# Value columns of a hybrid transformer trunk projected token-major, 512 columns at a time, and kept in DRAM

## The chip, the cores and the metric

The kernel runs on one core of a Trainium2 chip. The metric is the device time of one execution in microseconds (us). The engines are TensorE (PE in the profile, with PEld for its weight loads), VectorE (DVE), ScalarE (ACT), GpSimd (POOL) and SyncE (SP), which issues nearly all DMAs. Each engine works through its own queue of instructions in order.

## The reference

Two layers over 512 latent and 256 context tokens of width 2048. The layers share one shape; layer 1 needs the context tokens only where latent tokens read them (recurrent gates and values, attention keys and values).

```python
h  = rms_norm(x, norm_w) * (1.0 + scale[:, None]) + shift[:, None]   # shift, scale, gate = silu(c) @ ada_w + ada_b
hc = rms_norm(xc, norm_w) * (1.0 + scale_c) + shift_c
(a_u, a_v, a_z, b_q, b_i, b_ff, b_fb, b_z, c_q, c_k, c_v, c_z) = split_columns(h @ w_in)
y_a = gmlp_branch(a_u, a_v, a_z, g_ln_w, g_ln_b, g_ws, g_bs)      # 4 heads of 128; gelu, layer norm, mixing over tokens
y_b = hgrn_output(ox_f + flip(ox_b), b_z, h_norm_w)               # 4 recurrent heads, forward and backward, values b_i
y_c = diff_output(o_lat, c_z, subln_w, lam_init)                  # 4 heads of differential attention, values c_v (256 wide)
y = jnp.concatenate([y_a, y_b, y_c], axis=-1) @ w_out
x_new = x + gate[:, None] * y
```

After the second layer comes a final RMS norm. All values are float32.

## The kernel before, in words

**Numbers.** Every float32 operand of a projection is split into a high and a low part of the type fp32r (`hi`, `lo` for activations; `wh`, `wl` for weights), and a product is three matmuls: hi·wh, lo·wh, hi·wl. Splitting is a copy on ACT (L318) and a subtraction on DVE (L319) for each weight tile of 128 x 512. The activations of a layer stay in SBUF as 16 k-tiles (`hi0` to `hi15`, `lo0` to `lo15`), each 128 features by 768 tokens.

**Jobs.** The input projection is cut into jobs of one column tile (128 columns of `w_in`). `Proj` keeps the weights stationary and streams the tokens, 512 and then 256 columns at a time: 16 k-tiles x 3 products x 2 widths, 96 matmuls (L148). A recurrent head (`Hgrn`) has five jobs: two gates, query, output gate and value `bi`. An attention head (`Attn`) has eight: two each of `cz`, `ck`, `cv`, `cq`. Gated MLP (`Gmlp`) has ten: four `au`, two for its values, four `az`. Its two value jobs are of another kind, `TokProj` (L374): activations stationary, weights moving 256 wide, so that the result has tokens on the partitions. The values of the recurrent heads and of attention come out of `Proj` with features on the partitions and are turned by six transposes on PE for each column tile (`transpose_all`, L497), copied and split.

**Order.** The first four jobs (`LEAD`) run together while the activations are being made; the rest run one after another, with the next job's weights fetched ahead. Behind the projections of head 0 of the recurrent unit run its seven *levels* (`Hgrn.levels`): for each, ACT copies keys (L569), PE does 24 (layer 0) or 16 (layer 1) small matmuls (L581; the trace counts each twice), DVE merges them (L590) and scales queries (L599), POOL scales keys (L601, L603) and totals (L604). Then `mix` (L636 to L667) combines scores, states and values, and `finish` transposes the result. Tile gives each engine one fixed order of instructions, made when the program is built.

**Buffers.** PSUM has two pairs of banks under the tag `pp` (one `Proj` each) and four single banks under the tag `a1`, for which everything small queues up: levels, mix, transposes, the filler's last matmul. `wh` and `wl` have five buffers each, `adas` two.

**Fillers.** The modulation vectors of later layers are worked out on DVE beside the projections (`ada_dve`): a block is 16 steps of two operations (L275, L277), a transpose, a reduction (`red`) and four small matmuls on PE (L288). After each job `advance` lets some steps through: `FILL` per kind of unit.

Of the kernel before, what the change touches and what calls it, by code (L numbers as in the profile page):

```python
# [47 lines left out]
def trunk(  # L48
    ctx: ExitStack,
    tc: tile.TileContext,  # L50
    xT, cc, ada_w, w_in, w_out, ws, bs, pack, rope, out,
# [288 lines left out]
    def tok_weights(src):  # L340
        out = []
        for g in range(8):
            raw = wp.tile([P, 2, 2, P], F32, tag="raw", bufs=5, name=nm("raw"))
            load(
                raw.rearrange("p c k n -> p c (k n)"),
                src[:, :, 2 * g : 2 * g + 2, :].rearrange("c p k n -> p c (k n)"),
            )
            wh = wp.tile([P, 2, 2 * P], F32R, tag="wh", bufs=5, name=nm("wh"))
            wl = wp.tile([P, 2, 2 * P], F32R, tag="wl", bufs=5, name=nm("wl"))
            split_into(  # L350
                wh.rearrange("p k (c n) -> p k c n", c=2),
                wl.rearrange("p k (c n) -> p k c n", c=2),
                raw.rearrange("p c k n -> p k c n"),
            )
            out.append((wh, wl))
        return out

    class TokProj:
        def __init__(self, nch):
            self.nch = nch  # L360
            self.banks = [(0, 4, ps.tile([P, 4, 2 * P], F32, tag="pp", bufs=2, name=nm("pp")))]
            if nch > 4:
                self.banks.append((4, 6, p_one([P, 2, 2 * P])))

        def mm(self, ws, acts):
            for g, (wh, wl) in enumerate(ws):
                for k in range(2):
                    kt = 2 * g + k
                    hi, lo = acts[kt]
                    for a, b, bank in self.banks:  # L370
                        for c in range(a, b):
                            cs = slice(c * P, (c + 1) * P)
                            for i, (x, w) in enumerate(((hi, wh), (hi, wl), (lo, wh))):
                                PE.matmul(  # L374
                                    bank[:, c - a, :],
                                    x[:, cs],
                                    w[:, k, :],
                                    start=(kt == 0 and i == 0 and c % 2 == 0),
                                    stop=(kt == KT - 1 and i == 2),
                                    skip_group_check=True,  # L380
                                )
# [18 lines left out]
    yscr = [[dp.tile([P, T], F32, tag=f"y{l}_{j}", name=f"y{l}_{j}") for j in range(12)] for l in range(DEPTH)]  # L400
    xscr = [dp.tile([P, T], F32, tag=f"x1_{j}", name=f"x1_{j}") for j in range(KT)]
# [283 lines left out]
    class Attn:  # L685
# [4 lines left out]
        def jobs(self):  # L690
            h = 2 * self.hd
            out = []
            for key, ctxn, fn in (("cz", False, self.out_gate), ("ck", True, self.key), ("cv", True, self.value), ("cq", False, self.query)):
                if False:
                    out.append((COL[key] + h, ctxn, fn, "tok"))
                    continue
# [511 lines left out]
```

## Time and profile before

| | |
|---|---|
| time, median of three runs | 2842.38 us (2838.59 to 2842.87) |
| profiled execution, own time | 2844.0 us |
| its span | 2842.1 us |
| PE busy | 2774.2 us (98%) |
| PEld, DVE, ACT, POOL busy | 85%, 56%, 34%, 11% |
| chain that ended last | PE 91%, of it L148 into pp 73% |
| DMA queue of SP | 313.27 MB, 38.1% of 16 engines' span |

The span is what the trace shows; some 1.9 us of the execution lie around it. A busy share counts a matmul from start to its modelled end, and matmuls overlap, so the time that a matmul costs in a dense stream is the distance from its start to the next one's. The chain follows the work back from the last instruction; where it names PE, PE was neither idle nor waiting.

### The profile page before, as it was taken

Reading aid. Unit: us, or ns where it says so; the run is one execution under the profiler, and the core shown is the slowest. Engines: PE = TensorE matmul, PEld = TensorE weight load, DVE = VectorE, ACT = ScalarE, POOL = GpSimd, SP = SyncE. Lnnn points to the kernel's source line nnn. Section 1 sums busy time; section 2 is a strip of 40 time slices with the busy share of each in tenths; the row PEclk is TensorE's granted clock in tenths of the full one; section 3 lists DMA queues with packets and bytes.
Section 4 is the critical chain, followed back from the end, with each engine's and each line's share of the span. In section 5 each row is a group of like instructions: output and inputs, shape, how many; then the busy total and the mean of one; then the engine's idle time right before and its main releaser. Section 6 shows DMA issues by size and latency. Waiting matters only on the chain.

```text
span 2842.1 us, 47179 instructions
## 1 busy us (share of the span) xinstructions
PE 2774.2 (98%) x18724; PEld 2401.6 (85%) x18724; DVE 1587.5 (56%) x3256; ACT 963.5 (34%) x1855; POOL 325.7 (11%) x307
## 2 busy tenths in 40 slices
PE   5989999999999999999999999999999999999997
PEld 3678888888888888898888888888888888889786
DVE  4475676767767576624768664334353535344434
ACT  3243233224343343322311243333253535342321
POOL 0033023000000000001011023233000000001122
PEclk9999999999999999999999999999999999999998
DMA  9833433443333334334645422222222222324543
GB/s 357 285 96 84 121 108 107 121 126 90 116 90 115 93 98 126 93 93 121 208 145 163 121 65 67 61 67 72 67 75 64 71 67 64 78 79 137 153 97 93
DMA packets 168862, 316.29 MB, mean 111 GB/s; under 512 B 18240, under 2 KB 32704, under 8 KB 168640
## 3 DMA queue, kind: packets, MB, share of 16 engines
q1 hardware_dynamic: 168640, 313.27, 38.1%
q8 instruction: 147, 2.41, 0.3%
q14 instruction: 75, 0.61, 0.1%
HBM read 294.85 MB, written 18.35 MB: 110 GB/s over the span
## 4 chain that ended last, share of the span: by engine, by line
PE 91%; issue 3%; DVE 2%; DMA 1%; POOL 1%; ACT 1%; SPq 0%; DVEq 0%; POOLq 0%; ACTq 0%
PE pp L148 73%; PE pp L374 3%; PE a L808 3%; PE a L769 2%; PE a L497 2%; PE a L148 2%; PE a L250 1%; PE a L374 1%; PE a L581 1%; PE a L659 1%; PE a L636 1%; POOL A L601 0%; POOL A L603 0%; DMA T<-y 0%; PE a L883 0%
## 5 line engine op out<-in xcount | busy, mean ns | idle before, releaser
L148 PE MATMUL pp<-hi,wh 128*128 128x512 f32 (+1 forms) x4016 | 1392.5, 348 | 5.5 <-ACT hi L311 2.8
L148 PE MATMUL pp<-lo,wh 128*128 128x512 f32 (+1 forms) x4016 | 1396.7, 348 | 0.5 <-DVE lo L312 0.2
L148 PE MATMUL pp<-hi,wl 128*128 128x512 f32 (+1 forms) x4016 | 1389.1, 346 | 0.0
L148 PEld LDWEIGHTS pp<-hi,wh 128*128 128x128 f32 x4016 | 759.5, 190 | 108.0 <-ACT hi L311 5.6
L148 PEld LDWEIGHTS pp<-lo,wh 128*128 128x128 f32 x4016 | 761.2, 190 | 99.0 <-issue 6.5
L148 PEld LDWEIGHTS pp<-hi,wl 128*128 128x128 f32 x4016 | 760.2, 189 | 90.6
L319 DVE TENSOR_TENSOR wl<-raw,wh 128x512 fp32r<-128x512 f32 x634 | 451.0, 713 | 675.6 <-ACT wh L318 653.7
L318 ACT CAST wh<-raw 128x512 fp32r<-128x512 f32 x634 | 392.3, 621 | 1192.6 <-PE pp L148 996.6
L277 DVE SCALAR_TENSOR_TENSOR acc<-adas,cc_s,acc 128x256 f32<-128x256 f32 x960 | 430.7, 498 | 72.2 <-DMA adas<-in_ada_w_dram 71.3
L817 POOL TENSOR_TENSOR ars<-e,mhalf 128x1 f32<-128x1 f32 x40 | 24.7, 617 | 1249.2 <-DVE e L815 1249.2
L780 ACT ACTIVATE C<-a,nb 128x256 f32<-128x256 f32 (+1 forms) x144 | 80.6, 566 | 54.5 <-DVE nb L776 47.7
L774 DVE TENSOR_REDUCE mx<-a 128x1 f32<-128x256 f32 (+1 forms) x144 | 72.7, 538 | 27.4 <-PE a L769 27.2
L808 PE MATMUL a<-A,WT 128*128 128x256 f32 x624 | 87.7, 282 | 0.0
L808 PEld LDWEIGHTS a<-A,WT 128*128 128x128 f32 x624 | 83.1, 191 | 3.8
L769 PE MATMUL a<-K,Q 128*128 128x256 f32 (+1 forms) x432 | 85.5, 336 | 0.0
L145 POOL TENSOR_TENSOR WT<-WT,T 128x768 f32<-128x768 f32 (+1 forms) x26 | 42.1, 1619 | 367.8 <-ACT T L144 367.8
L569 ACT COPY T<-A 128x768 f32<-128x768 f32 (+1 forms) x56 | 43.8, 782 | 95.2 <-POOL A L603 92.3
L769 PEld LDWEIGHTS a<-K,Q 128*128 128x128 f32 x432 | 68.1, 189 | 8.5
L705 ACT COPY T<-pp 32x512 f32<-32x512 f32 x128 | 74.1, 579 | 1.9
L374 PE MATMUL pp<-wh,hi 128*128 128x256 f32 x256 | 73.4, 287 | 0.1
L374 PE MATMUL pp<-wh,lo 128*128 128x256 f32 x256 | 73.1, 286 | 0.0
L374 PE MATMUL pp<-wl,hi 128*128 128x256 f32 x256 | 73.1, 286 | 0.0
(226 smaller groups left out, 2314.0 us busy)
## 6 DMA issues: line engine op xcount, KB each, us to landing
raw<-in_w_in_dram SPq DMA_DIRECT2D x512, 256.0 KB, 2.9
adas<-in_ada_w_dram SPq DMA_DIRECT2D x256, 256.0 KB, 2.9
raw<-in_w_out_dram SPq DMA_DIRECT2D x128, 256.0 KB, 3.0
adaw<-in_ada_w_dram SPq DMA_DIRECT2D x42, 384.0 KB, 7.1
K<-in_ada_w_dram SPq DMA_DIRECT2D x28, 384.0 KB, 6.6
T<-y SPq DMA_DIRECT2D x12, 384.0 KB, 4.9
A<-in_xT_dram SPq DMA_DIRECT2D x8, 384.0 KB, 6.0
B<-in_xT_dram SPq DMA_DIRECT2D x8, 384.0 KB, 6.3
```

The lines of the kernel that those rows point to most:

```text
L148: i = PE.matmul(*args, **kw)
L277: V.scalar_tensor_tensor(acc[:, i, :], wt[:, kt % 2, :], sca, acc[:, i, :], op0=ALU.mult, op1=ALU.add)
L318: S.copy(hi, src)
L319: V.tensor_tensor(lo, src, hi.bitcast(F32), op=ALU.subtract)
L374: PE.matmul(bank[:, c - a, :], x[:, cs], w[:, k, :], start=(kt == 0 and i == 0 and c % 2 == 0), stop=(kt == KT - 1 and i == 2), skip_group ...
L497: PE.transpose(pt[:, c - a, :], src[:, c * P : (c + 1) * P], ident)
L569: S.copy(km[:, :n].rearrange("p (j h i) -> p j h i", h=2, i=m), view(K2, 0, [[2 * m, n // (2 * m)], [T + m, 2], [1, m]]),)
L705: S.copy(sw[a : a + 32, :LAT], p[b : b + 32, :LAT])
L769: PE.matmul(pt[:, : hi - lo], a[:, qs], b[:, k0 + lo : k0 + hi], start=(i == 0), stop=(i == 2))
L774: V.tensor_reduce(mx[:, i : i + 1], pt[:, : hi - lo], axis=AX.X, op=ALU.max)
L780: S.activation(pr[:, m, lo:hi], pt[:, : hi - lo], AF.Exp, bias=nb, scale=SCALE, accum_out=sums[:, m, i : i + 1] if len(parts) == 2 else sm ...
L808: PE.matmul(po, a[:, c, :], b[:, c0 + c, :], start=(cnt == 0), stop=(cnt == 3 * nkc - 1))
```

## The change

The 16 value column tiles of a layer that belong together in fours are no longer jobs. `TOK` lists the first column tile of four *groups*: `bi` of the four recurrent heads, the first and second half of `cv`, and `av`. A `TokGroup` has activations stationary and weights moving 512 wide (L365 after the change), with one PSUM bank for each chunk of 128 tokens: six (four for gated MLP in layer 1). Two of the six are `a1` banks, four are the two `pp` pairs. It goes through 12 k-tiles chunk by chunk, then through the last four (`TOKLAST`) for one chunk after another. `store` copies each bank to SBUF on ACT (for gated MLP with Gelu) and writes it to DRAM. The four groups run behind the lead and the levels of head 0, before all other jobs. The units load their values from there later, and the six transposes of each value column go. The mix of head 0 now comes in the program behind group 0, and `prepare_rest` too. Of the fillers 24, 40, 40 and 40 steps are let through after the groups (`TOKFILL`), and `FILL` for a recurrent job is 7. The swap of the first two remaining jobs is gone. The lines after L147 have other numbers: 288, 319, 497, 554 and 581 of before are 289, 320, 498, 553 and 580 there.

```diff
+TOK = (16, 48, 52, 4)
...
-    class TokProj:
+    class TokGroup:
         def __init__(self, nch):
             self.nch = nch
-            self.banks = [(0, 4, ps.tile([P, 4, 2 * P], F32, tag="pp", bufs=2, name=nm("pp")))]
-            if nch > 4:
-                self.banks.append((4, 6, p_one([P, 2, 2 * P])))
+            self.banks = [p_one([P, 512]) for _ in range(nch - 4)]
+            for _ in range(2):
+                pair = ps.tile([P, 2, 512], F32, tag="pp", bufs=2, name=nm("pp"))
+                self.banks += [pair[:, 0, :], pair[:, 1, :]]
 
         def mm(self, ws, acts):
...
+            steps = [(kt, c) for kt in range(KT - TOKLAST) for c in range(self.nch)]
+            steps += [(kt, c) for c in range(self.nch) for kt in range(KT - TOKLAST, KT)]
+            for kt, c in steps:
+                hi, lo = acts[kt]
+                wh, wl = (w.rearrange("p c n -> p (c n)") for w in ws[kt])
+                cs = slice(c * P, (c + 1) * P)
+                for i, (x, w) in enumerate(((hi, wh), (hi, wl), (lo, wh))):
+                    PE.matmul(
+                        self.banks[c],
+                        x[:, cs],
+                        w,
...
+        def store(self, scr, func):
+            for c, bank in enumerate(self.banks):
+                t = g3("T3")
+                if func == AF.Copy:
+                    S.copy(t[:, :512], bank)
+                else:
+                    S.activation(t[:, :512], bank, func)
+                load(scr[:, c, :], t[:, :512])
...
-        def value(self, p):
-            raw = g3("T3")
-            p.act(raw, AF.Copy, T)
-            self.vt = vt = g3("K3", shape=(P, NCH, P))
-            for a, b, pt in transpose_all(raw, NCH):
-                V.tensor_copy(vt[:, a:b, :], pt[:, : b - a, :])
+        def last(self, p):
+            self.out_gate(p)
+            self.value()
+
+        def value(self):
+            self.vt = g3("K3", shape=(P, NCH, P))
+            load(self.vt, tscr[self.L.l][0][:, :, self.hd * P : (self.hd + 1) * P])
             self.mix()
             self.finish()
...
         def query(self, p, m):
             self.q[m] = self.rotate(p, self.L.n, "Q3")
+            if m == 0:
+                self.value()
...
         rest = jobs[LEAD:]
-        if SWAP:
-            rest[0], rest[1] = rest[1], rest[0]
-        nxt = fetch(rest[0])
+        nxt = tok_weights(w_tok[l, 0])
...
         u0.levels()
+        for i in range(4):
+            pt = TokGroup(NCH if i < 3 else L.nch)
+            pt.mm(nxt, acts)
+            nxt = tok_weights(w_tok[l, i + 1]) if i < 3 else fetch(rest[0])
+            pinned[0] = False
+            pt.store(tscr[l][i], AF.Copy if i < 3 else AF.Gelu)
+            if i == 0:
+                u0.value()
+                if l == 0:
+                    prepare_rest()
+            advance(fillers, TOKFILL[i])
```

How the change moves instructions is shown at three places. The numbers behind names tell buffers apart; `a1_`, `pp_` are PSUM banks, `wh_`, `wl_` weights, `hi`, `lo` activations.

First place: PE, levels of head 0 in layer 1. Before, around level 2 (L581):

```order
L148 MATMUL pp_2828_17649<-hi11_2758_17235,wl_2793_17409 128x256
L148 MATMUL pp_2828_17649<-hi12_2773_17286,wh_2795_17414 128x512
L581 MATMUL a1_2811_17486<-C6_2803_17436,T3_2810_17484 32x32 x16
L148 MATMUL pp_2828_17649<-lo12_2774_17287,wh_2795_17414 128x512
L148 MATMUL pp_2828_17649<-hi12_2773_17286,wl_2796_17415 128x512
L148 MATMUL pp_2828_17649<-hi13_2776_17313,wh_2795_17414 128x512
```

Between one level and the next stand some 24 matmuls of a job there. After the change, levels 1 to 6 (L580), the transposes of the keys (L498) and the first matmul of group 0 into an `a1` bank:

```order
L365 MATMUL pp_2855_17088<-wh_2786_16784,lo4_2714_16387 128x512
L580 MATMUL a1_2835_16922<-C6_2827_16872,T3_2834_16920 32x32 x16
L580 MATMUL a1_2837_16946<-C6_2827_16872,T3_2836_16944 32x32 x16
L580 MATMUL a1_2839_16970<-C6_2827_16872,T3_2838_16968 32x32 x16
L580 MATMUL a1_2841_16994<-C6_2827_16872,T3_2840_16992 32x32 x16
L580 MATMUL a1_2843_17021<-C6_2827_16872,T3_2842_17019 32x32 x16
L580 MATMUL a1_2845_17048<-C6_2827_16872,T3_2844_17046 64x64 x8
L498 MATMUL a1_2847_17064<-ident_75,A6_2822_16855 128x128 x4
L498 MATMUL a1_2848_17065<-ident_75,A6_2822_16855 128x128 x2
L498 MATMUL a1_2850_17075<-ident_75,A6_2822_16855 128x128 x4
L498 MATMUL a1_2851_17076<-ident_75,A6_2822_16855 128x128 x2
L365 MATMUL a1_2852_17085<-wh_2774_16760,hi0_2661_16171 128x512
```

Levels 1 to 6 now follow one another with nothing between. Ahead of these rows stand 60 matmuls of the group (k-tiles 0 to 4 into the four `pp` banks), 18 of them between level 0 and level 1. Layer 0 has the same picture: 24 matmuls, level 0, 25, level 1, 11, then levels 2 to 6 and the transposes.

Second place: PE, group 3 of layer 0. After the change, the end of its first 60 matmuls, the matmuls of two filler blocks (L289) and its first into an `a1` bank; the same form stands in group 2, with one block in place of two:

```order
L365 MATMUL pp_632_3538<-wh_556_3294,hi4_133_668 128x512
L365 MATMUL pp_632_3538<-wl_557_3295,hi4_133_668 128x512
L365 MATMUL pp_632_3538<-wh_556_3294,lo4_134_669 128x512
L289 MATMUL a1_611_3445<-red_610_3443,fold_80 32x4 x4
L289 MATMUL a1_623_3504<-red_622_3502,fold_80 32x4 x4
L365 MATMUL a1_629_3535<-wh_544_3270,hi0_77_374 128x512
L365 MATMUL a1_629_3535<-wl_545_3271,hi0_77_374 128x512
```

Before, a filler block's matmul (L288) stood among the matmuls of a job that need nothing of it, as here in layer 0:

```order
L148 MATMUL pp_537_3305<-hi14_259_1351,wh_525_3262 128x256
L497 MATMUL a1_508_3110<-ident_75,WT_493_3064 128x128 x4
L497 MATMUL a1_509_3111<-ident_75,WT_493_3064 128x128 x2
L288 MATMUL a1_531_3274<-red_530_3272,fold_80 32x4 x4
L148 MATMUL pp_537_3305<-lo14_260_1352,wh_525_3262 128x256
L148 MATMUL pp_537_3305<-hi14_259_1351,wl_526_3263 128x256
```

The second of the L289 reads `red_622`, the last row of the next fence. DVE's queue at the same place, after the change (L278 is L277 of before): the second of the two blocks, `acc_612`.

```order
L278 SCALAR_TENSOR_TENSOR acc_612_3451<-adas_613_3452,cc_s_86,acc_612_3451 128x256
L211 TENSOR_TENSOR adaT0_94<-a1_611_3445,pack_98 128x4
L278 SCALAR_TENSOR_TENSOR acc_612_3451<-adas_613_3452,cc_s_86,acc_612_3451 128x256
L278 SCALAR_TENSOR_TENSOR acc_612_3451<-adas_614_3458,cc_s_86,acc_612_3451 128x256 x4
L278 SCALAR_TENSOR_TENSOR acc_612_3451<-adas_615_3464,cc_s_86,acc_612_3451 128x256 x4
L278 SCALAR_TENSOR_TENSOR acc_612_3451<-adas_616_3470,cc_s_86,acc_612_3451 128x256 x4
L278 SCALAR_TENSOR_TENSOR acc_612_3451<-adas_617_3476,cc_s_86,acc_612_3451 128x256 x4
L278 SCALAR_TENSOR_TENSOR acc_612_3451<-adas_618_3482,cc_s_86,acc_612_3451 128x256 x4
L278 SCALAR_TENSOR_TENSOR acc_612_3451<-adas_619_3488,cc_s_86,acc_612_3451 128x256 x4
L278 SCALAR_TENSOR_TENSOR acc_612_3451<-adas_620_3494,cc_s_86,acc_612_3451 128x256 x4
L284 STREAM_TRANSPOSE T3_621_3500<-acc_612_3451 128x512
L286 TENSOR_REDUCE red_622_3502<-T3_621_3500 128x16
```

Ahead of these rows, and behind `wl_557` (the split of weight tile 4 of group 3), stands the first block, `acc_600`, in the same form: 32 operations, a transpose, a reduction. `wl_557` takes the buffer of `wl_504`, weight tile 15 of group 2. Before, the 32 operations of a block stood in twos, threes and fours among the work of a job:

```order
L277 SCALAR_TENSOR_TENSOR acc_532_3280<-adas_535_3293,cc_s_86,acc_532_3280 128x256 x2
L644 SCALAR_TENSOR_TENSOR Q3_492_3058<-Q3_492_3058,K3_422_2478,a1_490_3051 128x128
L277 SCALAR_TENSOR_TENSOR acc_532_3280<-adas_536_3299,cc_s_86,acc_532_3280 128x256 x2
L319 TENSOR_TENSOR wl_540_3405<-raw_538_3402,wh_539_3404 128x512
L277 SCALAR_TENSOR_TENSOR acc_532_3280<-adas_536_3299,cc_s_86,acc_532_3280 128x256 x2
L277 SCALAR_TENSOR_TENSOR acc_532_3280<-adas_550_3428,cc_s_86,acc_532_3280 128x256 x3
```

Third place: PE, the end of the mix of head 0 in group 1 of layer 0, after the change. Ahead of it stand 60 matmuls of the group and the mix's own; L498 transposes the mix's result, L425 and L289 belong to `prepare_rest` and to a filler block:

```order
L659 MATMUL a1_421_2282<-K3_402_2218,K3_321_1543 128x128
L659 MATMUL a1_421_2282<-Q3_405_2227,C6_319_1539 128x128
L498 MATMUL a1_424_2292<-ident_75,WT_409_2246 128x128 x4
L498 MATMUL a1_425_2293<-ident_75,WT_409_2246 128x128 x2
L425 MATMUL a1_427_2311<-lpr_426_2309,ones_82 128x2
L425 MATMUL a1_430_2321<-lpr_429_2319,ones_82 128x2
L289 MATMUL a1_447_2397<-red_446_2395,fold_80 32x4 x4
L365 MATMUL a1_453_2428<-wh_349_2106,hi0_77_374 128x512
```

`K3_402` are the values that the mix loads from DRAM. Before, the matmuls of a job stood between the mix and its transposes.

## Rows read from the trace of the kernel before

**Rows 1.** The page, parts 1 and 4: engines' busy time, chain by engine.
```profile
PE 2774.2 (98%) x18724; PEld 2401.6 (85%) x18724; DVE 1587.5 (56%) x3256; ACT 963.5 (34%) x1855; POOL 325.7 (11%) x307
...
PE 91%; issue 3%; DVE 2%; DMA 1%; POOL 1%; ACT 1%; SPq 0%; DVEq 0%; POOLq 0%; ACTq 0%
```
**Rows 2.** Windows: stretch, length, engines' busy us, granted clock, DMA share, GB/s.
```profile
139.14:142.55 3.41, 3.41 (x16) 1.36 (x10) 0.69 (x1) 0.62 (x1) 0.00 (x0) 0.50 0.90 324
1207.51:1210.92 3.41, 3.41 (x17) 3.08 (x17) 1.35 (x5) 3.38 (x7) 0.00 (x0) 0.50 0.47 120
160.00:215.00 55.00, 46.81 (x597) 40.03 (x597) 45.77 (x80) 23.93 (x43) 23.07 (x22) 1.00 0.40 122
1690.00:1740.00 50.00, 50.00 (x504) 42.60 (x503) 21.60 (x33) 20.43 (x40) 28.60 (x25) 1.00 0.28 65
```
**Rows 3.** Waits of PE: in total, times, longest (us).
```profile
PE a L581 <- DVE C L599: 5.8, 3, 2.5
PE a L250 <- DMA B<-in_ada_w_dram: 2.3, 1, 2.3
PE a L822 <- DVE ao L819: 2.1, 1, 2.1
```
**Rows 4.** Timeline of PE, 700 to 712: start, length, instruction, idle before.
```profile
700.33 0.39 PE L148 MATMUL pp<-hi,wl 128*128 128x512 f32 x1
...
702.61 0.28 PE L148 MATMUL pp<-hi,wh 128*128 128x256 f32 x1
...
704.04 0.40 PE L148 MATMUL pp<-hi,wh 128*128 128x512 f32 x1
...
704.74 0.82 PE L497 MATMUL a<-ident,C 128*128 128x128 f32 x6
...
705.62 0.39 PE L148 MATMUL pp<-lo,wh 128*128 128x512 f32 x1
```
**Rows 5.** Timeline of PE, 1215 to 1219.
```profile
1214.72 0.28 PE L374 MATMUL pp<-wh,lo 128*128 128x256 f32 x1
...
1217.85 0.28 PE L374 MATMUL pp<-wl,hi 128*128 128x256 f32 x1
```
**Rows 6.** The page, part 6: DMA issues, KB each, us from issue to landing.
```profile
adas<-in_ada_w_dram SPq DMA_DIRECT2D x256, 256.0 KB, 2.9
...
T<-y SPq DMA_DIRECT2D x12, 384.0 KB, 4.9
...
y<-WT SPq DMA_DIRECT2D x4, 384.0 KB, 2.5
```
**Rows 7.** Timeline of ACT in the levels of layer 1.
```profile
1718.57 0.62 ACT L569 COPY T<-A 128x512 f32<-128x512 f32 x1 [1.98 <-POOL A L603]
```
**Rows 8.** Timeline of POOL, the same level.
```profile
1719.51 0.84 POOL L601 TENSOR_TENSOR A<-A,K 128x384 f32<-128x384 f32 x1
1720.31 0.84 POOL L603 TENSOR_TENSOR A<-A,K 128x384 f32<-128x384 f32 x1
```
**Rows 9.** Timeline of POOL in the levels of layer 0.
```profile
178.38 0.98 POOL L601 TENSOR_TENSOR A<-A,B 128x384 f32<-128x384 f32 x1
179.32 1.10 POOL L603 TENSOR_TENSOR A<-A,B 128x384 f32<-128x384 f32 x1
```
**Rows 10.** Timeline of ACT, the same level.
```profile
180.45 0.84 ACT L569 COPY T<-A 128x768 f32<-128x768 f32 x1 [1.32 <-POOL A L603]
```
**Rows 11.** Timeline of PE, mix of head 0 in layer 0.
```profile
223.73 2.39 PE L636 MATMUL a<-K,Q 128*128 128x128 f32 x20
...
245.61 0.82 PE L497 MATMUL a<-ident,WT 128*128 128x128 f32 x6
```
**Rows 12.** Timeline of DVE, filler operations of a later block.
```profile
442.56 1.67 DVE L277 SCALAR_TENSOR_TENSOR acc<-adas,cc_s,acc 128x256 f32<-128x256 f32 x4
445.18 1.67 DVE L277 SCALAR_TENSOR_TENSOR acc<-adas,cc_s,acc 128x256 f32<-128x256 f32 x4 [0.95 <-DMA adas<-in_ada_w_dram]
```
**Rows 13.** Groups of DVE: count, busy us, mean ns, idle before.
```profile
L283 DVE STREAM_TRANSPOSE T<-acc 128x512 f32<-128x512 f32 x32 | 22.6, 705 | 0.3
```

More of the change, by code (lines that the diff above doesn't have):

```diff
@@ L50, in trunk @@
     tc: tile.TileContext,
[L51 removed]
+    xT, cc, ada_w, w_in, w_tok, w_out, ws, bs, pack, rope, out,
 ):
@@ L341, in tok_weights @@
         out = []
[L342 to L355, printed above, removed]
+        for kt in range(KT):
+            raw = wp.tile([P, 4, P], F32, tag="raw", bufs=5, name=nm("raw"))
+            load(raw.rearrange("p c n -> p (c n)"), src[kt])
+            out.append(w_split(raw))
@@ L365, in mm @@
         def mm(self, ws, acts):
[L366 to L381, printed above, removed]
+            steps = [(kt, c) for kt in range(KT - TOKLAST) for c in range(self.nch)]
@@ new lines, in mm @@
+            steps += [(kt, c) for c in range(self.nch) for kt in range(KT - TOKLAST, KT)]
[8 more added lines that the diff above has]
+                        w,
+                        start=(kt == 0 and i == 0),
+                        stop=(kt == KT - 1 and i == 2),
+                        skip_group_check=True,
+                    )
@@ L400, in trunk @@
     yscr = [[dp.tile([P, T], F32, tag=f"y{l}_{j}", name=f"y{l}_{j}") for j in range(12)] for l in range(DEPTH)]
+    tscr = [[dp.tile([P, NCH, 512], F32, tag=f"t{l}_{g}", name=f"t{l}_{g}") for g in range(4)] for l in range(DEPTH)]
     xscr = [dp.tile([P, T], F32, tag=f"x1_{j}", name=f"x1_{j}") for j in range(KT)]
@@ L509, in jobs @@
                 (COL["bq"] + h, False, self.query),
-                (COL["bz"] + h, False, self.out_gate),
+                (COL["bz"] + h, False, self.last),
             ]
-            out.append((COL["bi"] + h, True, self.value))
-            return out
         def gate(self, p, d):
@@ L692, in jobs @@
             out = []
[L693 to L696, printed above, removed]
+            for key, ctxn, fn in (("cz", False, self.out_gate), ("ck", True, self.key), ("cq", False, self.query)):
                 for m in range(2):
@@ L832, in jobs @@
         def jobs(self):
-            v = [(COL["av"] + 2 * j, False, lambda p, j=j: self.value(p, j), "tok") for j in range(2)]
             u, z = (
@@ L904, in up @@
             p.act(self.u[h], AF.Gelu, n)
+            if h == 0:
+                self.value()
+            if h == 3:
+                self.mix()
         def out_gate(self, p, h):
@@ L945, in run_layer @@
         lead = jobs[:LEAD]
-        is_tok = lambda j: len(j) > 3
-        fetch = lambda j: tok_weights(w_in[l, j[0] : j[0] + 2]) if is_tok(j) else weights(w_in[l, j[0]])
+        fetch = lambda j: weights(w_in[l, j[0]])
         pts = []
@@ L997, in run_layer @@
         u0.levels()
[L998 to L1005 removed]
+        for i in range(4):
[9 more added lines that the diff above has]
+            advance(fillers, TOKFILL[i])
+        for i, j in enumerate(rest):
+            pt = Proj(width(j))
+            for g in range(4):
+                mm_group(pt, nxt[g], acts, g)
             nxt = fetch(rest[i + 1]) if i + 1 < len(rest) else weights(w_out[l, 0])
@@ L1162, in wtiles @@
         return w.reshape(l, k // P, P, n // P, P).transpose(0, 3, 2, 1, 4)
+    w_in = wtiles(a["w_in"])
+    w_tok = np.stack([w_in[:, c : c + 4] for c in TOK], 1).transpose(0, 1, 4, 3, 2, 5)
     small = dict(
```

69 lines of the change are left out of this document (24 added, 45 removed).

## Prediction

> **What bounds the kernel now.** I read the page first: its engine line and its chain say that TensorE (PE) is nearly all there is [rows 1]. PE is busy for 98% of the span, and 91% of the chain that ended last is PE work. So a change counts in two ways only: by the time that its matmuls take in the stream, and by new waits of PE. The busy column can't price the first, since matmuls overlap; I take distances between starts in the timeline. For the second I read which stretches have gaps today. Between 160 and 215 us, where head 0 of the recurrent unit runs its seven levels in layer 0, PE lacks 55.00 − 46.81 = 8.2 us; the same place of layer 1 (1690 to 1740) has no gap at all [rows 2]. Those gaps are short (three of them 5.8 us together) and wait for VectorE's (DVE's) C of L599 [rows 3]: a level's matmuls come due before the chain behind them is ready. Nearly everything else runs dense, so a chain that loses its cover of matmuls will show in full.
>
> **What the change removes on PE.** Ten matmuls of 512 columns start 702.61 − 700.33 = 2.28 us apart, 0.228 us each; twelve of 256 take 704.04 − 702.61 = 1.43 us, 0.119 each [rows 4]. The token-major 256s of before (L374) take (1217.85 − 1214.72)/26 = 0.120 [rows 5]; between the two rows shown lie 25 of their kind. Before, 12 value columns a layer (4 bi, 8 cv) cost 48 matmuls of each width, 1152 of each over both layers, and gated MLP 16 × 3 × 2 × (6 + 4) = 960 of 256. After, 16 × 3 × (24 + 22) = 2208 of 512 do the same. So 1056 more of 512 at 0.228 (+240.8) and 2112 fewer of 256 (1152 × 0.119 + 960 × 0.120 = 252.3): **−11.5 us**. If the weights as moving side ran at 0.230, it would be −9.4. The value transposes go: 24 groups of six. Such a group lies at 704.74; from 704.04 to 705.62 are 1.58 us for four matmuls of 512 columns, which take 0.92 without it, so 0.66 us each [rows 4], 24 × 0.66 = **−15.8 us**. Together −27.
>
> The Trainium skill ("TensorE: Matmul & The Clock Gate", section "Back-to-back issue gap") has a start-to-start time of columns/2.4 GHz + 2.5 ns, so 216 ns for 512 and 109 for 256; an estimate by that page is 1056 × 0.216 − 2112 × 0.109 = −2 us for the first term, and a sum 9 us higher. The trace has 228 and 119 instead, so halving the count pays more here.
>
> **What it adds off PE.** ScalarE copies banks out and casts weights either way, DVE splits either way; neither is near full (34% and 56% [rows 1]), so I cost them at nothing as long as PE has matmuls to run. A store of 384 KB lands 2.5 us after issue, a load of 384 KB from the same kind of scratch after 4.9 [rows 6]. For heads 1 to 3, attention and gated MLP the loads are asked for at least a job ahead or have the next job's 96 matmuls (48 × 0.347 = 16.7 us) as cover: nothing. If that cover were gone, each would cost some 5 to 10 us.
>
> **What it moves: six places.** A group needs two banks of the tag a1 besides the four of pp, and the order shows that they are handed out behind all earlier users of a1. Until then PE has only the four pp banks, and with five weight buffers only k-tiles 0 to 4: 60 matmuls, 13.7 us. What stands ahead of the first a1 matmul in PE's queue holds all the rest.
>
> *Levels, layer 1.* Levels 2 to 6 and the transposes stand with no matmul between them. One turn is a copy on ScalarE (0.62 [rows 7]) and two products on GpSimd (0.84 each [rows 8]), some 2.45 us with the handovers. From level 0 six turns (14.7) and a tail of one copy and two products (2.3) make 17; cover is 18 matmuls (4.1) and the levels' own matmuls (some 2): **+11 us**. Below, 6 (the products run two turns ahead, as they may); above, 16 (cover lost).
>
> *Levels, layer 0.* A turn is 0.84 + 0.98 + 1.10 and handovers, 3.05 us [rows 9, 10]; 6 × 3.05 + 2.9 = 21.2, less 36 matmuls (8.2) and the levels' own (3), are 10 us of gaps where there are 8.2 today: **+2 us**. Bounds −3 (no DVE filler stands between the levels now, and that made some of today's gaps) and +8.
>
> *Mix of head 0, layer 0,* now in group 1. Banks copied out, store 2.5, load 4.9: the values are there some 9 to 10 us after group 0. From the mix's first matmul to the transposes of its result are 21.9 us today (223.73 to 245.61 [rows 11]) with matmuls between; 16 filler operations still stand between its DVE steps, so I take 20. That is 30 us against 60 matmuls and the mix's own (19 in all): **+11 us**, between 6 (the matmuls that stretched the chain are gone) and 14.
>
> *Mix, layer 1.* No filler there: 16 × 0.42 = 6.7 us less of chain: **+3 us**, 0 to 6.
>
> *Group 2, layer 0.* The small matmul L289 of a whole filler block stands ahead of its a1 banks, and DVE does that block behind the split of weight tile 4, which waits for group 1's end. A filler pair of k-tiles (four operations) takes 1.67 us on DVE, and 445.18 − 442.56 = 2.62 where it waits for its load [rows 12]; two buffers and a load of 2.9 us [rows 6] allow 2.2 to 2.6. Eight pairs, two of them loaded already: 6 × 2.4 + 2 × 1.7 + transpose, reduction and split (2.8) = 20.6, less 13.7: **+7 us**; 3 with DVE alone, 8 with every load late.
>
> *Group 3, layer 0.* Two whole blocks stand there, acc_600 and acc_612, again behind weight tile 4 (wl_557): 64 operations. With DVE alone 16 × 1.67 + two transposes and reductions (0.7 each [rows 13], 2.8) + 0.7 = 30.2; with 2.3 a pair 40. I take 38, nearer the rows with loads, since stores and weights now stand in the same queue: 38 − 13.7 = **+24 us**, bounds 14 and 27.
>
> Waits: 11 + 2 + 11 + 3 + 7 + 24 = 58.
>
> *The clock.* After waits of 2.1 and 2.3 us (L822, L250 [rows 3]) TensorE had stretches of 3.41 us at half clock (1.2 GHz), granted 0.50 (139.14 and 1207.51), but none in 160 to 215, where it waited 2.5 us and resumed [rows 2]. A stretch costs half of itself, 1.7 us; five new waits above 3 us: **+9**, between 0 and 17 (double stretches).
>
> The Trainium skill says in the same page (section "Loop structure matters more than you think") that long waits between matmuls drop the clock, which speaks against this change; the rows at 139 and 1207 agree with it, the row of 160 to 215 shows that not every wait does it.
>
> **Sum.** −27 + 58 + 9 = +40 us on the profiled execution, 2844.0 (span 2842.1 and 1.9 around it): 2884. That execution lies 1.6 us above the median of 2842.38, so 2882. Low bounds: waits −3 + 6 + 6 + 0 + 3 + 14 = 26, clock 0, net −1. High: 8 + 16 + 14 + 6 + 8 + 27 = 79, clock 17, net +69.
>
> **Rivals.** 0.2%, 5.7 us, is about what a measurement here tells from no change.
>
> *The waits are half as long* (chance 0.20): chains run ahead where I count them from level 0, and filler loads keep up. Waits and clock of 21 to 47: 2836 to 2862, of it 0.08 within 0.2%. For it: GpSimd's and ScalarE's steps of a level don't need PE. Against: DVE's 64 operations alone leave 16 us at group 3.
>
> *Only the removal shows* (0.13): faster. The mechanism is that DVE does the filler blocks before the groups end, so L289 finds its sums ready, and levels and mixes cost what they do now: −27 + 11 of the mixes gives 2826. It decides when all waits and clock together stay under 27 − 6 = 21. For it: DVE is busy for 56% only [rows 1]. Against: it is an in-order queue, and wl_557 there can't run before group 2 gives its buffer back.
>
> *The round trip is late* (0.05): value loads queue on SP behind stores that wait for ScalarE's copies, and attention or gated MLP wait too: one wait of 10 us in a layer more, 20 and a clock stretch each: 2905 to 2920.
>
> *The forecast* (0.62): 2862 to 2910. Faster 0.13, same 0.08, slower 0.12 + 0.62 + 0.05 = 0.79. The range 2836 to 2910 leaves out the second rival and most of the third.
>
> **What would show it.** In the profile of after: L365 starts 0.228 us apart; no value transposes; PE waits ahead of L289 for DVE's red in groups 2 and 3 of layer 0, 7 and 24 us; L580 with 2.4 to 3 us between levels 2 to 6; a wait of some 10 us at the mix of head 0; half clock behind them; from head 1 on as dense as now. It is wrong if the first a1 matmul of group 3 comes within 20 us of group 2's end, or if new waits stand in attention.

## The result, and the profile after

The changed kernel takes 2912.64 us, median of four runs (2910.09 to 2915.8), against 2841.16 for the kernel before: ratio 1.0253, 95% interval 1.0235 to 1.0271. It is 71.5 us slower. The forecast was 40 slower, and the range ended at 2910. The profiled execution has a span of 2909.1 us, 67.0 more than before, and a mean granted clock of 0.977.

The page of after, its parts 1, 2 and 4 (busy time, the span in 40 slices, chain by engine), beside [rows 1]:

```profile
PE 2769.5 (95%) x17524; PEld 2353.5 (81%) x17524; DVE 1579.1 (54%) x3224; ACT 967.7 (33%) x1852; POOL 328.5 (11%) x307
...
PE   5988997999999999999999998999999999999997
...
PEclk9989998999999999999999999999999999999998
...
PE 84%; DVE 5%; DMA 5%; issue 4%; ACT 1%; POOL 1%; SPq 0%; DVEq 0%; POOLq 0%; ACTq 0%
```

PE's busy time is hardly less, its share of the chain fell from 91% to 84%, and DVE and DMA took up the difference. The waits of PE after (in total, times, longest, us), beside [rows 3]:

```profile
PE a L289 <- DVE red L286: 34.2, 5, 17.3
...
PE a L580 <- ACT T L568: 10.2, 5, 2.6
...
PE a L580 <- DVE C L598: 7.9, 6, 1.7
PE a L498 <- DVE WT L667: 7.0, 2, 3.5
PE a L659 <- DVE Q L644: 4.5, 3, 2.3
...
PE pp L365 <- DVE T L484: 3.1, 1, 3.1
PE pp L149 <- DVE T L484: 2.9, 1, 2.9
```

The largest is the one before the filler's small matmuls (L289). In group 3 of layer 0 (timeline of PE: start, length, instruction, idle before) the 60 matmuls into pp end, and then:

```profile
439.31 0.29 PE L289 MATMUL a<-red,fold 128*32 128x4 f32 x8 [6.87 <-DVE red L286]
456.91 0.29 PE L289 MATMUL a<-red,fold 128*32 128x4 f32 x8 [17.31 <-DVE red L286]
457.12 0.80 PE L365 MATMUL a<-wh,hi 128*128 128x512 f32 x1
457.72 0.63 PE L365 MATMUL a<-wl,hi 128*128 128x512 f32 x1
458.15 0.63 PE L365 MATMUL a<-wh,lo 128*128 128x512 f32 x1
458.57 0.63 PE L365 MATMUL a<-wh,hi 128*128 128x512 f32 x1
```

24.2 us of waiting, and behind it matmuls that start 0.42 to 0.43 apart: half clock, 1.2 GHz. DVE at the same time goes through the two blocks:

```profile
443.28 3.30 DVE L278 SCALAR_TENSOR_TENSOR acc<-adas,cc_s,acc 128x256 f32<-128x256 f32 x8 [1.16 <-DMA adas<-in_ada_w_dram]
447.66 3.33 DVE L278 SCALAR_TENSOR_TENSOR acc<-adas,cc_s,acc 128x256 f32<-128x256 f32 x8 [1.08 <-DMA adas<-in_ada_w_dram]
452.09 3.29 DVE L278 SCALAR_TENSOR_TENSOR acc<-adas,cc_s,acc 128x256 f32<-128x256 f32 x8 [1.10 <-DMA adas<-in_ada_w_dram]
455.42 0.71 DVE L284 STREAM_TRANSPOSE T<-acc 128x512 f32<-128x512 f32 x1
456.17 0.69 DVE L286 TENSOR_REDUCE red<-T 128x16 f32<-128x512 f32 x1
```

Two loads' worth (eight operations) come every 4.4 us, 2.2 a pair of k-tiles: the end of the reduction at 456.86 lets PE go on at 456.91.

Windows of after, over the six places (length, then PE's busy us first; the granted clock is the third number from the end):

```profile
172.80:204.15 31.35, 24.53 (x432) 20.22 (x433) 23.04 (x26) 11.38 (x22) 24.25 (x22) 0.79 0.16 49
267.90:290.10 22.20, 13.53 (x79) 12.13 (x77) 14.54 (x42) 2.46 (x14) 1.34 (x1) 0.76 0.21 65
350.00:365.00 15.00, 8.13 (x49) 6.24 (x48) 12.07 (x30) 0.00 (x0) 0.00 (x0) 0.89 0.40 123
425.60:457.20 31.60, 7.41 (x51) 5.84 (x46) 25.94 (x64) 0.00 (x0) 0.00 (x0) 0.68 0.39 118
550.00:580.00 30.00, 23.06 (x221) 20.02 (x221) 27.47 (x51) 5.21 (x7) 7.49 (x5) 0.94 0.43 132
1760.00:1780.20 20.20, 11.56 (x274) 9.54 (x272) 7.16 (x13) 6.65 (x17) 15.16 (x19) 0.78 0.01 2
1844.00:1855.20 11.20, 7.75 (x60) 7.19 (x58) 4.82 (x16) 1.47 (x8) 1.04 (x1) 1.00 0.00 0
```

Length less busy time gives PE's idle time: levels of layer 0 6.8 (8.2 before, [rows 2]), mix 8.7, group 2 6.9, group 3 24.2; in layer 1 levels 8.6 and mix 3.4. The row at 550 is head 1's levels, with 6.9 that were not forecast.

**Where 67 us of span went.** I add up all distances between successive starts on PE from the first to the last (2808.0 us before, 2875.9 after), take out the idle time that the trace gives before an instruction (34.3 and 107.0), and count what then lies in stretches of half clock (21.2 and 76.2) by half. What is left is an estimate of PE's work at full clock: 2763 before, 2731 after. So the work fell by 32, idle time rose by 73, and half clock took some 27: together 68.

### The profile page after: what moved, and what is told of

Same layout as the page of the kernel before. It is cut to its first block, busy times and chain, and to the rows that moved or that the text cites. A ratio compares the mean times of both kernels' runs of the same rounds, so it can differ in the third digit from the quotient of the medians.

```text
span 2909.1 us, 44897 instructions
## 1 busy us (share of the span) xinstructions
PE 2769.5 (95%) x17524; PEld 2353.5 (81%) x17524; DVE 1579.1 (54%) x3224; ACT 967.7 (33%) x1852; POOL 328.5 (11%) x307
## 4 chain that ended last, share of the span: by engine, by line
PE 84%; DVE 5%; DMA 5%; issue 4%; ACT 1%; POOL 1%; SPq 0%; DVEq 0%; POOLq 0%; ACTq 0%
PE pp L149 59%; PE pp L365 8%; PE a L365 5%; PE a L802 3%; PE a L763 2%; DVE acc L278 2%; DMA adas<-in_ada_w_dram 2%; PE a L149 1%; PE a L498 1%; PE a L251 1%; DMA adaw<-in_ada_w_dram 1%; PE a L580 1%; PE a L659 1%; DMA K<-in_ada_w_dram 1%; DVE wl L320 1%
## 5 line engine op out<-in xcount | busy, mean ns | idle before, releaser
L149 PE MATMUL pp<-hi,wh 128*128 128x512 f32 (+1 forms) x3248 | 1137.1, 352 | 8.4 <-ACT hi L312 3.1
L149 PE MATMUL pp<-lo,wh 128*128 128x512 f32 (+1 forms) x3248 | 1140.3, 352 | 0.6 <-DVE lo L313 0.5
L149 PE MATMUL pp<-hi,wl 128*128 128x512 f32 (+1 forms) x3248 | 1134.3, 350 | 0.0
L149 PEld LDWEIGHTS pp<-hi,wh 128*128 128x128 f32 x3248 | 616.9, 190 | 91.8 <-ACT hi L312 4.1
L149 PEld LDWEIGHTS pp<-lo,wh 128*128 128x128 f32 x3248 | 618.5, 191 | 82.5 <-issue 4.2
L149 PEld LDWEIGHTS pp<-hi,wl 128*128 128x128 f32 x3248 | 617.6, 190 | 76.1 <-issue 0.5
L278 DVE SCALAR_TENSOR_TENSOR acc<-adas,cc_s,acc 128x256 f32<-128x256 f32 x960 | 434.0, 502 | 78.7 <-DMA adas<-in_ada_w_dram 77.9
L365 PE MATMUL pp<-wh,hi 128*128 128x512 f32 x512 | 199.3, 392 | 3.1 <-DVE T L484 3.1
L365 PE MATMUL pp<-wl,hi 128*128 128x512 f32 x512 | 200.4, 391 | 0.0
L365 PE MATMUL pp<-wh,lo 128*128 128x512 f32 x512 | 200.3, 391 | 0.0
L365 PEld LDWEIGHTS pp<-wh,hi 128*128 128x128 f32 x512 | 96.6, 189 | 23.4 <-issue 3.3
L365 PEld LDWEIGHTS pp<-wl,hi 128*128 128x128 f32 x512 | 96.5, 189 | 20.0
L365 PEld LDWEIGHTS pp<-wh,lo 128*128 128x128 f32 x512 | 96.6, 189 | 19.9
L365 PE MATMUL a<-wh,hi 128*128 128x512 f32 x224 | 89.7, 405 | 0.0
L365 PE MATMUL a<-wl,hi 128*128 128x512 f32 x224 | 89.4, 399 | 0.0
L365 PE MATMUL a<-wh,lo 128*128 128x512 f32 x224 | 89.0, 397 | 0.0
```

The lines of the kernel that those rows point to most:

```text
L149: i = PE.matmul(*args, **kw)
L278: V.scalar_tensor_tensor(acc[:, i, :], wt[:, kt % 2, :], sca, acc[:, i, :], op0=ALU.mult, op1=ALU.add)
L365: PE.matmul(self.banks[c], x[:, cs], w, start=(kt == 0 and i == 0), stop=(kt == KT - 1 and i == 2), skip_group_check=True,)
```

## The experiments

All ratios are against the kernel before. Each edit is on the changed kernel unless said otherwise.

**e1, loads of the tables and first fillers in program order.** The SP timeline of after shows four loads among the first ones, which in the kernel before came behind the lead:

```profile
25.38 2.64 SPq L70 DMA_DIRECT2D raw<-in_w_in_dram  x4
28.68 0.33 SPq L70 DMA_DIRECT2D rope_c<-in_rope_dram  x1
29.65 0.33 SPq L70 DMA_DIRECT2D rope_s<-in_rope_dram  x1
30.69 1.47 SPq L70 DMA_DIRECT2D adas<-in_ada_w_dram  x2
```

They are the change's doing: it sets `pinned[0] = False`, which frees loads of program order, ahead of `prepare_rest` and the first `advance`, and the scheduler moves them forward.

```diff
                 if l == 0:
+                    pinned[0] = True
                     prepare_rest()
             advance(fillers, TOKFILL[i])
+            pinned[0] = False
```

> The changed kernel with one thing undone: the loads of the rope tables and of the first fillers are again kept in program order, so that the scheduler can't issue them among the first loads of the lead, where after the change four of them (1 MB) stand. Theory: they push the lead's own loads back where the DMA queue is full, and that is why the lead, whose code is the same, ends some 9.5 us later than before. Then the lead ends near 160 us again and the time is 2901 to 2905. Rival: the lead is later for another reason (scatter of the first loads, another order of its matmuls); then the time stays at 2910 to 2915 and the lead ends near 169.

Measured: 2918.5, ratio 1.0268 (1.0253 to 1.0283). Most of the lead's delay went, as the theory says, but not all: the first matmul of group 0 starts at 164.81 in place of 172.80, and the first job before the change at 161.19. The time did not follow. The first filler's loads now stand behind the store of head 0's mix, begin at 275.92 (timeline of SP, e1), and PE waits for that block ahead of group 1's a1 banks (timeline of PE, e1):

```profile
297.77 0.29 PE L289 MATMUL a<-red,fold 128*32 128x4 f32 x8 [24.22 <-DVE red L286]
```

Eight us won in the lead and 24 lost here: the same trap as in groups 2 and 3.

**e2, no fillers behind the groups.**

```diff
-    TOKFILL = (24, 40, 40, 40)
+    TOKFILL = (0, 0, 0, 0)
-    FILL = dict(Hgrn=7, Attn=7, Gmlp=4, Out=9)
+    FILL = dict(Hgrn=11, Attn=10, Gmlp=6, Out=9)
```

> The changed kernel with no filler steps behind the groups; they are spread over the later jobs instead (11, 10, 6 a job for recurrent heads, attention, gated MLP). Theory: the waits of 7 us in group 2 and of 7 + 17 us in group 3 go, and with them the half clock behind them (about 7 us); the time falls by 35 to 42 us to 2870 to 2878. Rival: DVE is short of time in the layer, the fillers' time comes back as waits in later jobs, and the time stays above 2890.

Measured: 2882.3, ratio 1.0145 (1.013 to 1.016), 30.3 us less. The waits for `red` went from 34.2 us to 1.5, as the theory says. The gain stayed 5 to 12 us short of it: the wait of the transposes for the mix (L498 for DVE's WT) rose from 7.0 to 12.3, and half clock fell only from 76.2 to 68.9 us. Neither theory alone.

**e3, levels and mix of head 0 behind the groups.**

```diff
-        u0.levels()
         for i in range(4):
...
+        u0.levels()
         for i, j in enumerate(rest):
...
+            if i == 1:
+                u0.value()
             j[2](pt)
```

> The changed kernel with the levels of head 0 behind the fourth group and its mix behind the second of the remaining jobs, in both layers; fillers as in the changed kernel. Theory: the waits between levels (some 10 us in layer 0, 8.6 in layer 1) shrink to those of before (7.5 and 0), those at the mix (8.7 and 3.4) go, and the half clock behind them too: 25 to 37 us less, 2876 to 2888. Rival 1: what counts is that the chains take as long as they do, and the waits only move to the new places: 2905 to 2915. Rival 2: the clock is lost anyway, and only the idle time comes back: 2890 to 2895.

Measured: 2884.06, ratio 1.0141 (1.0124 to 1.0158), 28.6 us less, as the theory says. The waits of L580 for ACT's copies fell from 10.2 to 1.7; those for `red` stayed (36.2).

**e4, all three.** The edits of e2 and e3, with `prepare_rest` moved behind group 3 and the tables and the fillers of the first two remaining jobs loaded in order.

```diff
+            if i == 3 and l == 0:
+                pinned[0] = True
+                prepare_rest()
+                pinned[0] = False
             advance(fillers, TOKFILL[i])
+        u0.levels()
...
             if i + 2 < len(rest):
+                pinned[0] = l == 0 and i < 2
                 advance(fillers, FILL[type(owner[i + LEAD]).__name__])
+                pinned[0] = False
```

> All three together: loads of the tables and first fillers kept in order, no fillers behind the groups, levels and mix of head 0 behind them. Theory: what is left of the change is the shorter stream on PE (27 us less by the prediction's working) and a few small waits: 2815 to 2832, faster than before. Rival: the removal is worth much less than 27 us (a 512 column matmul with moving weights costs as much as two of 256, or the stores, casts and loads take it back): 2838 to 2850, no faster than before.

Measured: 2865.19, ratio 1.008 (1.0065 to 1.0095). The theory failed: 47 us less than the changed kernel, but still 23 more than before. By the sum used above PE's work is 2825.9 − 68.6 − 53.5/2 = 2731, the same 32 us less than before, so the rival (the removal is worth little) falls too. What is left is idle time, 68.6 against 34.3, and half clock. The largest part of what is new lies in the recurrent heads (waits of PE, e4):

```profile
PE a L580 <- DVE C L598: 14.0, 8, 3.8
...
PE a L553 <- DVE WT L682: 3.7, 1, 3.7
```

Of the 14.0, 3.8 belong to head 0, whose levels e4 put above these jobs, 2.7 to head 3 of layer 1, the rest to heads 1 and 2 of layer 0. A head now has four jobs of matmuls in place of five above the same chain of levels and mix, but that alone does not make these waits: e5, below, has four jobs a head too, and waits for this C in head 3 of layer 1 alone. e4 also runs head 0's chain beside the other heads and lets 11 filler steps a job through in place of 7; e8 separates these two in part.

**e5, groups without a1 banks.** Each group goes over its weights twice, for four chunks of tokens and then for two, on the pp banks alone; all else as in the changed kernel.

```diff
     class TokGroup:
-        def __init__(self, nch):
-            self.nch = nch
-            self.banks = [p_one([P, 512]) for _ in range(nch - 4)]
-            for _ in range(2):
+        def __init__(self, a, b):
+            self.a, self.b = a, b
+            self.banks = []
+            for _ in range((b - a) // 2):
...
-        for i in range(4):
-            pt = TokGroup(NCH if i < 3 else L.nch)
+        passes = [(i, a, b) for i in range(4) for a, b in ((0, 4), (4, 6)) if i < 3 or a < L.nch]
+        for at, (i, a, b) in enumerate(passes):
+            pt = TokGroup(a, min(b, NCH if i < 3 else L.nch))
```

> The changed kernel with groups that use the pp banks alone: each group goes over its weights twice, first for four chunks of tokens, then for two, so the weights of those groups are loaded, cast and split twice; levels, mix and fillers stay where the change put them. Theory: what held PE in the first two groups and in groups 2 and 3 was that the a1 banks stand behind levels, mix and filler blocks in PE's order; without a1 the matmuls of the group stand between them, so of the 54 us of waits at the six places nearly all go, and 15 to 20 us of half clock with them; the lead stays 8 to 10 us late: 2832 to 2850. Rival: a second split of the weights takes DVE and ScalarE longer than the 22 us that two chunks give, and PE waits for wl: 2860 or more.

Measured: 2845.82, ratio 1.0016 (1.0007 to 1.0025), 67 us less than the changed kernel, with levels, mix and fillers where the change put them. That is the theory, and it settles what held PE: the order behind the a1 banks. Waits of PE, e5:

```profile
PE a L289 <- DVE red L286: 4.9, 3, 4.0
...
PE pp L365 <- DVE T L484: 3.1, 1, 3.1
...
PE a L580 <- DVE C L598: 2.7, 2, 1.7
PE pp L365 <- DVE wl L320: 2.7, 2, 2.4
```

The wait for `red` is 4.9 in place of 34.2, and the second split of the weights costs 2.7 of waiting. Half clock fell from 76.2 to 38.6 us and idle time from 107.0 to 54.2. PE's work by the sum above is 2812.8 − 54.2 − 38.6/2 = 2739, 8 more than in the changed kernel; why is open.

**e6, the same with the loads of e1.** On e5:

```diff
                 if l == 0:
+                    pinned[0] = True
                     prepare_rest()
             advance(fillers, TOKFILL[i])
+            pinned[0] = False
```

> As the one before, with the loads of the rope tables and of the first fillers kept in program order. Theory: the lead ends near 161 us as before the change, and since no a1 bank of a group waits for a filler block, nothing is held by the later filler: 8 to 10 us less than the one before, 2822 to 2842. Rival: the first filler block is late again and PE waits for it as in the first experiment: 2845 or more.

Measured: 2849.46, ratio 1.0027 (1.0017 to 1.0037): no gain. The wait of the first group fell from 3.1 to under 1, but the first filler is late again (10.4 us for `red`, 4.9 in e5), and weights too (5.2 for wl). The rival was right in kind, with a smaller wait than it said.

**e7, the price of the columns alone.** On e4, each matmul of a group as two of 256 columns.

```diff
-                    PE.matmul(
-                        self.banks[c],
+                    for hf in (slice(0, 256), slice(256, 512)):
+                        PE.matmul(
+                            self.banks[c][:, hf],
...
```

> The kernel with all three things undone (2865 us), with each matmul of a group as two of 256 columns: 4416 in place of 2208, nothing else changed. It measures the price of the columns alone. Theory: two of 256 take 2 x 0.1195 us where one of 512 takes 0.228, so 24 us more: 2885 to 2893. Rival: the width is worth next to nothing (two at 0.114): 2863 to 2872.

Measured: 2882.27, ratio 1.014 (1.0125 to 1.0155), 17.1 us more than e4: between the two. Its timeline of PE has a pair in 0.24 us:

```profile
200.26 0.40 PE L366 MATMUL pp<-wh,hi 128*128 128x256 f32 x2
200.50 0.40 PE L366 MATMUL pp<-wl,hi 128*128 128x256 f32 x2
```

where the changed kernel takes (231.86 − 224.83)/31 = 0.227 for one of 512 (30 of its kind lie between the two rows):

```profile
224.83 0.39 PE L365 MATMUL pp<-wh,hi 128*128 128x512 f32 x1
...
231.86 0.39 PE L365 MATMUL a<-wl,hi 128*128 128x512 f32 x1
```

13 ns a pair, times 2208, is 29 us, and PE's work by the sum above is 2843.3 − 57.4 − 54.4/2 = 2759, 28 more than e4. The time rose by less: idle time fell from 68.6 to 57.4. That the longer stream covers more of the chains is the likely reason; no run separates it.

**e8, fewer fillers in the recurrent heads.** On e4:

```diff
-    FILL = dict(Hgrn=11, Attn=10, Gmlp=6, Out=9)
+    FILL = dict(Hgrn=4, Attn=13, Gmlp=6, Out=9)
```

> The kernel with all three things undone (2865 us), with the fillers moved from the recurrent heads' jobs to attention's (4 and 13 a job in place of 11 and 10). It asks why that kernel still has some 20 us of waits in the recurrent heads of layer 0 that the kernel before doesn't have. Theory: a head has four jobs of matmuls in place of five over the same chain of levels and mix, and the fillers on DVE stretch that chain; with few fillers the waits of 430 to 690 us go: 2845 to 2855. Rival: the cover alone is too short, the waits stay: 2860 to 2870.

Measured: 2856.26, ratio 1.0051 (1.0036 to 1.0066), 8.9 less than e4. L580's waits for C fell from 14.0 to 8.1, but those of attention (L816 for DVE's ao) rose from 5.2 to 9.8: the waits moved with the fillers. In layer 0, 2.7 in head 0 and 2.7 in head 1 remained with only 4 steps a job. Both accounts hold in part.

**e9, the groups as cover.** e5's groups, spread: bi behind the lead, the halves of cv behind the jobs of heads 1 and 2, av ahead of gated MLP; loads in order, fillers 0, 16, 16, 16 behind groups and 9 a job of heads and attention.

```diff
+    GROUPAT = {0: 0, 4: 1, 8: 2, 36: 3}
...
+        for at, j in enumerate(rest):
+            if at in GROUPAT:
+                i = GROUPAT[at]
+                items += [(i, 4, 6), (i, 0, 4)] if i < 3 or L.nch > 4 else [(i, 2, 4), (i, 0, 2)]
+            items.append((at, j))
```

> The groups on the pp banks alone again, but spread over the layer: bi behind the lead as in the change, the two halves of cv behind the jobs of heads 1 and 2 of the recurrent unit, av ahead of gated MLP; two chunks of tokens first, then four. The tables and first fillers are loaded in program order, and the fillers are 0, 16, 16, 16 steps behind groups and 9 a job of heads and attention. Theory: what was left in the version with pp banks alone were the late lead and waits in heads, attention's end and gated MLP's end, where the value jobs had been cover; with the groups as cover there the gain of the shorter stream shows: 2815 to 2832. Rival: the chains of heads and attention wait as long wherever the groups stand, or the second split of the weights costs what the stream gains: 2836 to 2850.

Measured: 2821.07, ratio 0.9925 (0.9913 to 0.9938): 21.7 us faster than before the change, 92 faster than the change. Its page, parts 1 and 4, and two of its waits of PE:

```profile
PE 2751.6 (98%) x17524; PEld 2336.3 (83%) x17524; DVE 1671.0 (59%) x3352; ACT 1044.4 (37%) x1983; POOL 334.5 (12%) x307
...
PE 88%; DMA 4%; DVE 4%; issue 2%; POOL 1%; ACT 1%; SPq 0%; DVEq 0%; ACTq 0%; POOLq 0%
```

```profile
PE a L580 <- DVE C L598: 2.7, 2, 1.7
PE a L289 <- DVE red L286: 1.9, 3, 1.0
```

By the sum above: idle 37.2 (34.3 before the change), half clock 35.3 (21.2), work 2788.2 − 37.2 − 35.3/2 = 2733, 30 less. The matmuls of this kernel are those of the changed one (x17524 in both). Several things differ from e6, which has the same banks and ordered loads and is 28 us slower. Idle time is 23 us less (60.1 to 37.2): 8.5 of it at the fillers' `red`, 5.2 at wl, and 4.5 and 4.0 at head 1's levels and attention's end, behind both of which e9 has a group.

**e10, the early loads alone, in the kernel before.**

```diff
+            pinned[0] = False
             j[2](pt)
             if l == 0 and i == 0:
                 prepare_rest()
-            if i == UNPIN:
-                pinned[0] = False
```

> The kernel before the change, with one thing of the change alone: loads are free of program order already ahead of the rope tables and the first fillers, so that these four loads (1 MB) stand among the first loads of the lead, as after the change. Theory: this alone makes the lead 8 to 10 us longer: 2849 to 2854. Rival: what made the lead late after the change is something else: 2840 to 2845.

Measured: 2847.17, ratio 1.0017 (1.0008 to 1.0026), 4.4 us more. The first job behind the lead (timeline of PE, e10) waits as the first group does after the change, and starts 5.3 us later than before (161.19):

```profile
166.47 0.47 PE L148 MATMUL pp<-hi,wh 128*128 128x512 f32 x1 [3.31 <-DVE T L483]
```

The cause is there, at half the size that was expected.

**e11, gated MLP's values alone, in the kernel before.** 512 columns, pp banks, old place, no DRAM.

```diff
-            v = [(COL["av"] + 2 * j, False, lambda p, j=j: self.value(p, j), "tok") for j in range(2)]
+            cut = ((4, 6), (0, 4)) if self.L.nch > 4 else ((0, 2), (2, 4))
+            v = [(COL["av"], False, lambda p, j=j: self.value(p, j), "tok", c) for j, c in enumerate(cut)]
```

> The kernel before the change, with one part of the change alone: the values of gated MLP by matmuls of 512 columns, at their old place and kept in SBUF, on the pp banks alone (two passes over the weights). 480 matmuls of 512 take the place of 960 of 256. Theory: 960 x 0.120 - 480 x 0.228 = 6 us less, nothing else moves: 2834 to 2838. Rival: the second split of 16 weight tiles a layer makes PE wait: 2842 to 2850.

Measured: 2837.58, ratio 0.998 (0.9971 to 0.9989), 5.1 us less, as the theory says.

## Why the prediction was right and wrong

**The direction and its cause were right.** PE waits where the order of the queues said, and e5 shows the reason: without the a1 banks, and with levels, mix and fillers at their places in the program, 67 of the 71 us are gone.

**The removal** was put at −27 and is some −32 by the sum of starts (2731; 2729 to 2739 in the other kernels with matmuls of 512). e7 and e11 check it: a pair of 256 costs 13 ns more than one of 512 (11 in the working), and the part of gated MLP gave 5.1 of 6. The rule weighed there for matmuls taken singly (columns over 2.4 GHz plus 2.5 ns, from the Trainium skill, "TensorE: Matmul & The Clock Gate", section "Back-to-back issue gap") would make a pair 3 ns dearer; the rows have 0.240 and 0.227 us, and the measurement decides. The working's side estimate of −9.4 for weights at 0.230 took only the 1056 added matmuls at that price; for all 2208 it is −7.1.

**The six waits** were put at +58 and are +50: levels of layer 0 −1.4 (forecast +2), of layer 1 8.6 (11), mixes 8.7 and 3.4 (11 and 3; the working's own 11 − 6.7 is 4), group 2 6.9 (7), group 3 24.2 (24). All are inside their bounds. For group 3 the pair of k-tiles took 2.2 us, not 2.3, so that part of the working was close.

**The step that failed is that nothing is added outside the six places** ("from head 1 on as dense as now", and "nothing" for loads that have matmuls as cover). Idle time there rose by 73 − 50 = 22 us: 6.9 at head 1's levels (550 to 580; 2.4 of it for a filler's `red`), 4.0 in the levels of head 3 in layer 1, 2.9 late in layer 1 (L149 for DVE's T of L484), some 7 in and right behind the lead, the rest in pieces of 1 to 2. Half clock stood behind these waits too. Windows of after, first the six rows that lie at the six places (two at layer 0's mix, none at layer 1's), then head 3 of layer 1 and the wait late in layer 1 (PE's busy time follows the length, the granted clock is third from the end):

```profile
194.33:204.57 10.24, 6.11 (x133) 5.82 (x134) 4.52 (x5) 6.49 (x15) 7.44 (x10) 0.50 0.01 2
276.25:283.08 6.83, 5.46 (x26) 5.16 (x26) 4.58 (x16) 1.47 (x8) 0.00 (x0) 0.50 0.26 79
286.49:293.32 6.83, 5.63 (x26) 4.92 (x27) 1.82 (x7) 0.57 (x3) 0.00 (x0) 0.50 0.16 60
361.58:368.41 6.83, 3.92 (x17) 3.17 (x18) 5.67 (x15) 0.62 (x1) 0.00 (x0) 0.50 0.42 118
436.68:460.57 23.89, 3.95 (x24) 3.21 (x25) 19.69 (x49) 0.48 (x1) 0.00 (x0) 0.50 0.41 122
1771.29:1781.53 10.24, 5.53 (x63) 5.07 (x64) 2.75 (x4) 5.60 (x15) 6.00 (x8) 0.50 0.02 3
2221.85:2228.68 6.83, 5.89 (x62) 5.00 (x54) 2.70 (x4) 4.09 (x11) 2.36 (x5) 0.50 0.01 2
2709.95:2716.78 6.83, 6.10 (x14) 4.50 (x15) 4.10 (x7) 2.88 (x5) 0.00 (x0) 0.50 0.96 334
```

PE's busy time in the first six rows is 30.6 us, by half 15. So of the 27 us of half clock 12 lie elsewhere, mostly behind waits that the working put at nothing. The six places alone would have made −32 + 50 + 15 = 33 us, near the forecast of 40.

The working asked whether loads have cover and not what the value jobs themselves had covered. e4 (all six places mended, and still slower) shows that the rest counts, but not what it is, since it crowds head 0's chain into the other heads. The better sign is e9: with groups behind head 1 and attention, the waits of e6 there are gone, while head 3 of layer 1, which has no group behind it, waits as after the change, and not at all in the kernel before (timelines of PE, after and e9):

```profile
2219.89 0.46 PE L580 MATMUL a<-C,T 128*32 128x32 f32 x32 [1.71 <-DVE C L598]
```

```profile
2093.19 0.46 PE L580 MATMUL a<-C,T 128*32 128x32 f32 x32 [1.71 <-DVE C L598]
```

No run moves one group alone.

**The clock at the six places was put too low:** one stretch of 3.41 us for each of five waits, +9, between 0 and 17, where 15 came. The working took the shortest stretch of before as the price, and counted only waits above 3 us. There are 17 stretches in place of 6, most of 6.83 us and more, and a chain of small waits (levels, mix) holds the clock down as a long one does. The count by half is an upper estimate for places where PE has only small matmuls.

**A part of the change was not seen at all:** the line that frees loads of program order moved ahead of `prepare_rest`. The order of SP's queue showed it (four loads among the first 38), and the working asked of that queue only about values and weights. It delays the start of the first group by 8 us (e1), and in the kernel before costs 4.4 us alone (e10). After the change the first group starts 11.6 us later than the first job did; what of the remaining 3 to 4 is the lead's own other order of matmuls stays open.

Together: −32 + 73 + 27 = 68 of span against a forecast of −27 + 58 + 9. Of the 28 us of difference 34 come from places held to be covered or not looked at (22 of idle time, 12 of half clock) and 6 from the clock at the six places; 8 and 5 on the other side are the smaller waits and the larger removal. That the time lies only 3 us beyond the range is in part luck: without these 13 it would lie further out.

## What to carry to other kernels

Moving work from the middle of a pipeline to its front gives back its own time at once and takes away cover from every chain that ran beside it; ask of each removed matmul what waited behind it unseen. A tile that needs a shared pool of banks inherits everything that is queued for that pool, so a long accumulation belongs on banks that nothing small uses, even if its weights must be loaded and split twice (e5: 67 us won, for 2.7 us of waiting and some 8 of work). Read the DMA queue's order as closely as the engines', for a line that frees loads can act 100 us ahead of where it stands.

## What the runs showed of the hardware

Half clock came in stretches of 3.41 to 23.89 us after the change. Chains of waits of only 1.4 to 1.9 us each in the levels (192 to 200, clock 0.50 from 194.33) brought it as well, while in the kernel before three waits of up to 2.5 us among many matmuls there did not [rows 2, 3]. The Trainium skill ("TensorE: Matmul & The Clock Gate", section "Loop structure matters more than you think") warns of long waits between matmuls; the trace agrees at group 3, where matmuls start 0.42 to 0.43 us apart behind the wait of 17.3 us. By the count by half the clock took some 27 us here, nearly as much as the removal gave. Where the DMA queue was full at the start, loads of 256 KB took 7.1 to 7.5 us from issue to landing, against 2.9 over the run [rows 6].
